# The expert gather's first chunks in PSUM banks B, and the one-hot slots ahead of three low parts

## The chip, the cores and the metric

The kernel runs on one core of a Trainium2 chip. The metric is the device time of one execution in microseconds (us); lower is better. A core has five engines that run side by side, each through its own list of instructions in order: TensorE (PE in the profile; its weight loads are listed apart as PEld), VectorE (DVE), ScalarE (ACT), GpSimd (POOL) and SyncE (SP), which here issues the DMAs that bring the weights. They wait for one another through semaphores. Products of PE land in PSUM, which has eight banks of 128 partitions x 512 fp32 numbers.

## What is computed

Two layers over 256 tokens of width 1024: gated linear attention in the first, differential attention in the second, and after either a mixture of 16 experts with a two-level router:

```python
g_idx = argmax(t @ w_group + b_group)               # one of 4 groups for each token
top_w, top_i = top_k(softmax(e_logits[g_idx]), 2)   # 2 of its 4 experts
for e in range(16):
    hdn = silu(t @ w_gate[e]) * (t @ w_up[e])       # 1024 -> 512
    y = y + combine[:, e:e + 1] * (hdn @ w_down[e]) # 512 -> 1024
h = layer_norm(ALPHA * h + y)
```

## The kernel before, in words

The change lies in the mixture of experts, `moe(layer, ...)`, which runs once for each layer. The 256 tokens lie in two blocks of 128 partitions. The router's comparisons give each token its place in each expert's list (`posm`). An expert gets 64 slots; a later, short block takes what doesn't fit (in layer 1 one such block runs as a seventeenth expert, with its slots beside those of group 3).

**One-hot slots.** For each group of four experts, `one_hot(g)` (L515) compares `posm` with a row of numbers and makes `OH`, a 0/1 matrix of 128 tokens x 256 slots for each of the two token blocks: two DVE instructions.

**Split.** The tokens' activations `xa` are used as a sum of two parts of lower precision. `split_x(k)` (L529) makes them for one chunk `k` of 128 columns: ACT copies the high part into half of a tile `xs` (L534), DVE subtracts it from `xa` for the low part (L535). There are four `xs` tiles; chunk 4 takes the tile of chunk 0 when the products of chunk 0 are done.

**Gather.** `gather_group(g)` (L538) multiplies: for each of the 8 chunks four products (L553), high part with block 0's and block 1's slots, then low part with both, add up to 128 columns x 256 slots of the gathered, transposed tokens. Two chunks (k = 0 and 1, 2 and 3, ...) share one PSUM bank. Then the pair is scaled and shifted out of PSUM into `xg`: the even chunk by DVE (L562), the odd one by ACT (L560). ACT's evacuation of a pair waits for DVE's. In group 3 of layer 1 a chunk has 320 columns (the seventeenth expert's slots too) and takes a bank alone; L558 is its extra evacuation.

**Banks.** PSUM's eight banks are shared out by name: four `pA` hold the output sums `y` through the whole loop; two `pB` and two `pC` go round. Before the change the gather takes `pC` alone, so its third pair waits until the first pair is evacuated. In the loop over experts `pB` takes the gate/up products (`gu_part`, L610) and half of the down products (`down_part`, L638); `pC` takes the other half, and the small transposes of `s_prep` (L594) and `tr_part` (L626), whose results DVE copies out (L597, and `ht` at L629) and ACT reads once more (L600). A bank is given again to whoever asks next, when the reader of its last content is done.

**Order.** The first group is gathered at the start of `moe`, right behind the router; groups 1 to 3 at experts 4, 8 and 12, behind the transposes of the expert before. Their `OH` and the split of their first four chunks are made ahead; chunks 4 to 7 are split inside the gather. The framework's scheduler orders each engine's list; `after(x)` holds an instruction behind another. At the start the code says four `split_x`, then `one_hot(0)`, `gather_group(0)`, then `combine()` (the experts' weights, a chain of small DVE instructions and one exponential on ACT). The weights come through a ring of 16 tiles `W`; a tile's next load is issued by SP when PE has used it. L181 are products with zeros that keep PE busy, and L670 adds an expert's result to `y`.

Of the kernel before, what the change touches and what calls it, by code (L numbers as in the profile page):

```python
# [43 lines left out]
def body(ctx, tc, x, w_in, wa_out, kv_w, wq, wb_out, wg, wu, wd, gate2, rows, rtab, lng, lnb, cblob, pblob, onehot, out):  # L44
    nc = tc.nc
    pe, act, dve, pool, sp = nc.tensor, nc.scalar, nc.vector, nc.gpsimd, nc.sync
# [10 lines left out]
    def nm(s):  # L57
        uid[0] += 1
        return f"{s}{uid[0]}"
# [4 lines left out]
    def pB():  # L64
        return psum.tile([128, 512], F32, tag="B", bufs=2, name=nm("pB"))

    def pC():
        return psum.tile([128, 512], F32, tag="C", bufs=2, name=nm("pC"))

    def sm(shape, tag, dt=F32, bufs=2):  # L70
        return small.tile(shape, dt, tag=tag, bufs=bufs, name=nm(tag))
# [218 lines left out]
    def spare_tile(i, shape, dt, name):  # L290
        return spare.tile(shape, dt, tag=f"x{i}", bufs=1, name=name)
# [177 lines left out]
    def moe(layer, M, lg, rstd, nr, fold, side=None):  # L469
        with tc.tile_pool(name=f"moe{layer}", bufs=1) as mp:  # L470
# [42 lines left out]
            after = lambda i: tc.issue_after(getattr(i, "ins", i)) if i is not None else contextlib.nullcontext()  # L513

            def one_hot(g):  # L515
                n = 5 if layer and g == 3 else 4
                OH[g] = mp.tile([128, 2, n, 64], F32R, tag="OH", bufs=2, name=nm("OH"))
                for b in range(2):
                    mm = dve.tensor_tensor(OH[g][:, b, 0:4],
                                      posm[:, b, 4 * g:4 * g + 4].unsqueeze(2).broadcast_to([128, 4, 64]),  # L520
                                      iota.unsqueeze(1).broadcast_to([128, 4, 64]), op=ALU.is_equal)
                    if n == 5:
                        dve.tensor_scalar(OH[g][:, b, 4], iota, extra[1][:, b:b + 1], None, op0=ALU.is_equal)
                return mm
            gcol, bcol = P_G + 16 * layer, P_B + 16 * layer

            lows = []

            def split_x(k, eng, hold=None):  # L529

                t = mp.tile([128, 2, 2, 128], F32R, tag="xs", bufs=4, name=nm("xs"))
                x_ = xa[:, :, k * 128:k * 128 + 128]
                with after(hold):
                    act.activation(t[:, 0], x_, AF.Copy)  # L534
                lows.append(eng.tensor_sub(t[:, 1], x_, t[:, 0]))  # L535
                return t

            def gather_group(g, hold=None, xs=()):  # L538

                n = 5 if layer and g == 3 else 4  # L540
                t = mp.tile([128, KC, 256], F32, tag="xg", bufs=1, name=nm("xg"))
                if n == 5:
                    tx = spare_tile(1, [128, KC, 64], F32, "xg4")
                    xg_tiles[4] = tx
                xs = list(xs)
                for k in range(KC):
                    if n == 5 or k % 2 == 0:
                        p = pC()
                    if k >= len(xs):
                        xs.append(split_x(k, dve, hold))  # L550
                    o = p[:, 0:320] if n == 5 else p[:, k % 2 * 256:k % 2 * 256 + 256]
                    for q in range(4):
                        pe.matmul(o, xs[k][:, q // 2, q % 2], OH[g][:, q % 2].rearrange("p e s -> p (e s)"), start=q == 0, stop=q == 3)  # L553
                    for i in range(k, k + 1) if n == 5 else (k - 1, k) if k % 2 else ():
                        src = p[:, 0:256] if n == 5 else p[:, i % 2 * 256:i % 2 * 256 + 256]
                        gc, bc = (pb[:, c + i:c + i + 1] for c in (gcol, bcol))
                        if n == 5:
                            dve.tensor_scalar(tx[:, i], p[:, 256:320], gc, bc, op0=ALU.mult, op1=ALU.add)  # L558
                        if n == 5 or i % 2:
                            act.activation(t[:, i], src, AF.Identity, scale=gc, bias=bc)  # L560
                        else:
                            dve.tensor_scalar(t[:, i], src, gc, bc, op0=ALU.mult, op1=ALU.add)  # L562
                xg_tiles[g] = t
# [173 lines left out]
            def overflow(left, base, rev):  # L737
# [18 lines left out]
                ht, _ = tr_part(act_part(p, 2), 2)  # L756
                scatter(st, down_part(wdn, ht, wsx, 2)[0], True)

            xs0 = [split_x(k, dve) for k in range(4)]
            act.activation(sm([128, 2], "warm"), xs0[3][:, 0, 0, 0:2], AF.Exp, scale=0.0)  # L760
            one_hot(0)
            gather_group(0, None, xs0)
            with after(lows[3]):
                cw = combine()
            prev = None
            for e in range(E + layer):
                g = min(e // 4, 3)
                if e in (4, 8, 12):
                    with after(held[e][1]):
                        one_hot(g)  # L770
                    gather_group(g, held[e][0])
# [3 lines left out]
                p = pB()  # L775
# [50 lines left out]
            if layer == 0:  # L826
                p = pB()
# [187 lines left out]
    for j in range(2):  # L1015
# [9 lines left out]
        else:  # L1025
            t = mp.tile([128, 2, 4, S], F32R, tag="xhi", name="ogT1")
# [8 lines left out]
    def mask():  # L1035
        pool.memset(late["T"][0:64, :, 192:256], 1e30)

    moe(0, M0, *rt_, mask)


    with tc.tile_pool(name="mix1", bufs=1) as mp:
# [111 lines left out]
        xt1 = lambda h, b: xtq[:, b] if h else mp.tile([128, 4, 128], F32, tag="sc", bufs=2, name=nm("xts"))  # L1153
        rt_ = out_norm(mp, 1, late["o"], lambda k: (ohi[:, k], olo[:, k]), lambda k: gsub[:, 0:1], xt1)
    moe(1, M1, *rt_)


# [60 lines left out]
```

## Time and profile before

| | us |
|---|---|
| median of 3 runs (769.76 to 772.49) | 770.43 |
| the profiled execution | 771.24 |
| its span, first to last instruction | 769.3 |
| PE busy / DVE busy / ACT busy | 727.1 / 357.4 / 296.8 |

A row of a timeline gives start, duration, engine, line, what is written and read, how many instructions are merged, and in brackets the idle time before and who ended it. A row `x14` of products is 14 issued back to back; its duration runs from the first start to the last end. A 64-column product of an expert appears twice in the trace (`x2` for one row of the program). "PEclk" is the granted share of TensorE's full clock.

### The profile page before, as it was taken

How to read it: one execution, taken by the hardware profiler on the slowest of the kernel's cores; microseconds unless marked ns; L12 is line 12 of the kernel's file. 1: busy time of each engine (PE TensorE's matmuls, PEld its weight loads, DVE VectorE, ACT ScalarE, POOL GpSimd, SP SyncE). 2: the span in 40 equal slices, each digit the busy share in tenths (PEclk: the TensorE clock that was granted, in tenths of full speed). 3: DMA queues.
4: the chain of work that ended last, by engine and by line, in shares of the span. 5: the costliest groups of instructions: out<-in, count | busy, mean ns of one | idle time of the engine just before them, and what ended most of it. 6: DMA issues, size and time to landing. Idle time of an engine off the chain costs nothing. (4 is left out here: it accounts for less than half of the span.)

```text
span 769.3 us, 10560 instructions
## 1 busy us (share of the span) xinstructions
PE 727.1 (95%) x3743; PEld 407.8 (53%) x3743; DVE 357.4 (46%) x959; ACT 296.8 (39%) x651; POOL 8.9 (1%) x21
## 2 busy tenths in 40 slices
PE   7999998999999999999999999999999999999993
PEld 5898776434333434434798877753343343343331
DVE  3655766333263332322758877654235332332225
ACT  4554766323212322222666656552232232232123
POOL 2200000000000000000000000000000000000000
PEclk9999999999999999999999999999999999999997
DMA  7999957599999999999999355619999999999951
GB/s 226 312 384 388 337 191 262 181 397 394 367 387 392 393 396 395 393 393 367 290 364 359 111 174 209 220 62 389 394 381 395 393 363 384 395 395 393 392 200 55
DMA packets 131934, 247.57 MB, mean 322 GB/s; under 512 B 7932, under 2 KB 38117, under 8 KB 131750
## 3 DMA queue, kind: packets, MB, share of 16 engines
q1 hardware_dynamic: 131270, 244.68, 87.6%
q0 software_dynamic: 176, 1.59, 0.5%
q8 instruction: 31, 0.51, 0.3%
q10 hardware_dynamic: 432, 0.59, 0.2%
q14 instruction: 25, 0.20, 0.1%
HBM read 245.77 MB, written 2.63 MB: 323 GB/s over the span
## 5 line engine op out<-in xcount | busy, mean ns | idle before, releaser
L610 PE MATMUL pB<-W,xg 128*64 128x512 f32 x1056 | 263.6, 600 | 0.0
L610 PEld LDWEIGHTS pB<-W,xg 128*64 128x64 f32 x1056 | 77.3, 138 | 137.9 <-issue 132.3
L638 PE MATMUL pB<-W,ht 128*64 128x512 f32 x248 | 112.6, 594 | 0.0
L638 PE MATMUL pC<-W,ht 128*64 128x512 f32 x248 | 111.5, 592 | 0.0
L647 DVE SCALAR_TENSOR_TENSOR o<-pB,wst,o 64x512 fp32r<-64x512 f32 x31 | 23.1, 744 | 145.3 <-ACT o L646 145.3
L119 DVE TENSOR_TENSOR lo<-W,hi 128x512 fp32r<-128x512 f32 x96 | 66.4, 696 | 37.0 <-PE pA L128 23.9
L118 ACT ACTIVATE hi<-W 128x512 fp32r<-128x512 f32 x96 | 59.3, 629 | 48.3 <-PE pA L129 27.8
L646 ACT ACTIVATE o<-pB,wst 64x512 fp32r<-64x512 f32 x31 | 21.2, 682 | 129.6 <-PE pC L638 101.8
L619 DVE TENSOR_TENSOR hd<-sl,pB 128x256 f32<-128x256 f32 x33 | 13.9, 421 | 102.5 <-ACT sl L617 102.5
L617 ACT ACTIVATE sl<-pB 128x256 f32<-128x256 f32 x33 | 12.7, 385 | 126.0 <-PE pB L610 126.0
L638 PEld LDWEIGHTS pB<-W,ht 128*64 128x64 f32 x248 | 33.3, 137 | 52.4 <-issue 49.3
L553 PE MATMUL pC<-OH,xs 128*128 128x256 f32 (+1 forms) x256 | 39.7, 308 | 7.4 <-DVE ht L629 3.8
L670 PE MATMUL pA<-o,st 128*128 128x512 f32 x132 | 40.9, 431 | 4.3 <-DVE o L664 2.1
L553 PEld LDWEIGHTS pC<-OH,xs 128*128 128x128 f32 x256 | 34.8, 203 | 17.8 <-DVE ht L629 5.2
L638 PEld LDWEIGHTS pC<-W,ht 128*64 128x64 f32 x248 | 33.9, 137 | 19.4 <-issue 18.2
L670 PEld LDWEIGHTS pA<-o,st 128*128 128x128 f32 x132 | 22.4, 191 | 33.3 <-issue 23.5
L129 PE MATMUL pA<-x1Thi,lo 128*128 128x256 f32 x128 | 36.1, 288 | 1.4 <-DVE lo L119 1.2
L127 PE MATMUL pA<-x1Thi,hi 128*128 128x256 f32 x128 | 36.7, 288 | 0.0
L128 PE MATMUL pA<-x1Tlo,hi 128*128 128x256 f32 x128 | 36.2, 284 | 0.0
L128 PE MATMUL pA<-lo,xThi 128*128 128x384 f32 (+1 forms) x96 | 34.3, 357 | 0.0
L129 PE MATMUL pA<-hi,xTlo 128*128 128x384 f32 (+1 forms) x96 | 34.3, 357 | 0.0
L127 PE MATMUL pA<-hi,xThi 128*128 128x384 f32 (+1 forms) x96 | 34.2, 362 | 0.0
(338 smaller groups left out, 1086.2 us busy)
## 6 DMA issues: line engine op xcount, KB each, us to landing
W<-in_moe_w_gate_dram SPq DMA_DIRECT2D x132, 512.0 KB, 11.2
W<-in_moe_w_up_dram SPq DMA_DIRECT2D x132, 512.0 KB, 11.0
W<-in_moe_w_down_dram SPq DMA_DIRECT2D x66, 1024.0 KB, 12.0
W<-in_a_w_in_dram SPq DMA_DIRECT2D x16, 256.0 KB, 5.6
W<-in_a_w_in_dram SPq DMA_DIRECT2D x4, 1024.0 KB, 17.8
W<-in_a_w_out_dram SPq DMA_DIRECT2D x4, 1024.0 KB, 14.4
W<-in_kv_w_dram SPq DMA_DIRECT2D x4, 1024.0 KB, 8.8
W<-in_b_w_q_dram SPq DMA_DIRECT2D x16, 256.0 KB, 5.4
```

Source lines behind the costliest of these rows:

```text
L118: act.activation(hi, src, AF.Copy)
L119: dve.tensor_sub(lo, src, hi)
L127: pe.matmul(o, l[0], r[0], start=first, stop=False, skip_group_check=skip)
L128: pe.matmul(o, l[0], r[1], start=False, stop=False, skip_group_check=skip)
L129: pe.matmul(o, l[1], r[0], start=False, stop=last, skip_group_check=skip)
L553: pe.matmul(o, xs[k][:, q // 2, q % 2], OH[g][:, q % 2].rearrange("p e s -> p (e s)"), start=q == 0, stop=q == 3)
L610: mm = pe.matmul(p[c * m:c * m + m, 0:2 * fw].rearrange("p (g f) -> p g f", g=2), xg(k), w[:, :, kk, c * fw:c * fw + fw], start=k == 0, st ...
L619: anchor[1] = dve.tensor_mul(h, sl, p[:, fw:2 * fw])
L638: mm = pe.matmul(p[2 * c // nt][c * m:c * m + m, 0:w], ht[:, q % n, (q // n) * m:(q // n) * m + m], wd_[q // 2][:, q % 2, c * w:c * w + w] ...
L646: act.activation(hi, src, AF.Copy, scale=ws[a:a + m, 0:1])
L647: dve.scalar_tensor_tensor(lo, src, ws[a:a + m, 0:1], hi, op0=ALU.mult, op1=ALU.subtract)
L670: mm = pe.matmul(y[b][c], st[:, b * 128:b * 128 + 128], o[c], start=False, stop=last, skip_group_check=True)
```

## The change

Two edits. The gather takes its banks in turn: pairs 0 and 1 in `pB`, pairs 2 and 3 in `pC` (in the wide group chunks 0, 1 in `pB`, 2, 3 in `pC`, 4, 5 in `pB`, 6, 7 in `pC`). And at the start of `moe` only chunk 0 gets its low part ahead; the low parts of chunks 1 to 3 are made after both halves of `OH`.

```diff
-            def split_x(k, eng, hold=None):
+            def split_x(k, eng, hold=None, later=False):
...
-                lows.append(eng.tensor_sub(t[:, 1], x_, t[:, 0]))
+                low = lambda: lows.append(eng.tensor_sub(t[:, 1], x_, t[:, 0]))
+                if later:
+                    return t, low
+                low()
                 return t
...
                 for k in range(KC):
                     if n == 5 or k % 2 == 0:
-                        p = pC()
+                        i = k if n == 5 else k // 2
+                        p = pC() if i // 2 % 2 else pB()
...
-            xs0 = [split_x(k, dve) for k in range(4)]
+            xs0, rest = [split_x(0, dve)], []
+            for k in range(1, 4):
+                t, low = split_x(k, dve, later=True)
+                xs0.append(t)
+                rest.append(low)
             act.activation(sm([128, 2], "warm"), xs0[3][:, 0, 0, 0:2], AF.Exp, scale=0.0)
-            one_hot(0)
+
+            with after(one_hot(0)):
+                for low in rest:
+                    low()
             gather_group(0, None, xs0)
```

The lists of PE, DVE and ACT change in the eight gathers and nowhere else; those of SP and POOL stay as they were. Line numbers move: L553 becomes L558, L560 L565, L562 L567, L610 L615.

DVE at the start of layer 0's experts, behind `posm` (`xs` rows are low parts, `mx`, `ex`, `comb` belong to `combine`). Before:

```order
L519 TENSOR_TENSOR OH_1710<-posm_1694,cb 128x256
L535 TENSOR_TENSOR xs_1696<-xa,xs_1696 128x256
L535 TENSOR_TENSOR xs_1699<-xa,xs_1699 128x256
L535 TENSOR_TENSOR xs_1702<-xa,xs_1702 128x256
L535 TENSOR_TENSOR xs_1705<-xa,xs_1705 128x256
L519 TENSOR_TENSOR OH_1710<-posm_1694,cb 128x256
L568 TENSOR_REDUCE mx_1770<-lg_1645 128x10
L570 TENSOR_TENSOR ex_1772<-lg_1645,mx_1770 128x40
L574 SCALAR_TENSOR_TENSOR comb_1775<-rank_1681,ex_1772 128x32
L578 TENSOR_REDUCE s_1779<-ex_1772 128x2
L576 TENSOR_REDUCE sg_1777<-comb_1775 128x8
L535 TENSOR_TENSOR xs_1737<-xa,xs_1737 128x256
```

And now:

```order
L519 TENSOR_TENSOR OH_1707<-posm_1694,cb 128x256
L535 TENSOR_TENSOR xs_1696<-xa,xs_1696 128x256
L519 TENSOR_TENSOR OH_1707<-posm_1694,cb 128x256
L535 TENSOR_TENSOR xs_1699<-xa,xs_1699 128x256
L535 TENSOR_TENSOR xs_1701<-xa,xs_1701 128x256
L535 TENSOR_TENSOR xs_1703<-xa,xs_1703 128x256
L573 TENSOR_REDUCE mx_1770<-lg_1645 128x10
L567 TENSOR_SCALAR xg_1713<-pB_1714,pb 128x256
L575 TENSOR_TENSOR ex_1772<-lg_1645,mx_1770 128x40
L567 TENSOR_SCALAR xg_1713<-pB_1725,pb 128x256
L535 TENSOR_TENSOR xs_1737<-xa,xs_1737 128x256
```

The second half of `OH` stands three low parts earlier, and chunk 4's low part (`xs_1737`) now stands behind the evacuations of both first pairs instead of ahead of them; most of `combine` moves behind all low parts.

PE at expert 4 of layer 0, from the transposes of expert 3 on (L553 is the gather, L610 the gate/up product of expert 4). Before:

```order
L594 MATMUL pC_1999<-ident_r,ohw_1996 128x128 x2
L626 MATMUL pC_2006<-ident_r,hd_1990 128x128 x2
L553 MATMUL pC_2015<-OH_2011,xs_2016 128x256 x4
L553 MATMUL pC_2015<-OH_2011,xs_2023 128x256 x4
L553 MATMUL pC_2032<-OH_2011,xs_2033 128x256 x4
L553 MATMUL pC_2032<-OH_2011,xs_2040 128x256 x4
L610 MATMUL pB_2083<-W_992,xg_2014 64x512
L553 MATMUL pC_2049<-OH_2011,xs_2050 128x256 x4
L553 MATMUL pC_2049<-OH_2011,xs_2057 128x256 x4
```

And now:

```order
L599 MATMUL pC_1999<-ident_r,ohw_1996 128x128 x2
L631 MATMUL pC_2006<-ident_r,hd_1990 128x128 x2
L558 MATMUL pB_2015<-OH_2011,xs_2016 128x256 x4
L558 MATMUL pB_2015<-OH_2011,xs_2023 128x256 x4
L558 MATMUL pB_2032<-OH_2011,xs_2033 128x256 x4
L558 MATMUL pB_2032<-OH_2011,xs_2040 128x256 x4
L558 MATMUL pC_2049<-OH_2011,xs_2050 128x256 x4
L558 MATMUL pC_2049<-OH_2011,xs_2057 128x256 x4
L558 MATMUL pC_2066<-OH_2011,xs_2067 128x256 x2
L615 MATMUL pB_2083<-W_992,xg_2014 64x512
L558 MATMUL pC_2066<-OH_2011,xs_2067 128x256 x2
```

The first four chunks write `pB`, and the expert's first product, which stood behind chunk 3, now stands in the middle of chunk 6 and takes the `pB` bank in which chunks 0 and 1 were added up.

## Rows read from the trace of the kernel before

**Rows 1.** The page, busy time of the engines over the span.
```profile
PE 727.1 (95%) x3743; PEld 407.8 (53%) x3743; DVE 357.4 (46%) x959; ACT 296.8 (39%) x651; POOL 8.9 (1%) x21
```

**Rows 2.** PE's waits over the whole span: us in total, times, longest.
```profile
PE pC L553 <- DVE ht L629: 3.8, 6, 0.6
PE pC L553 <- DVE OH L519: 2.2, 2, 1.1
...
PE pC L553 <- ACT xg L560: 1.3, 3, 0.6
```

**Rows 3.** Timeline of PE at the start of layer 0's experts.
```profile
134.27 3.36 PE L553 MATMUL pC<-OH,xs 128*128 128x256 f32 x14 [1.12 <-DVE OH L519]
...
138.65 2.18 PE L553 MATMUL pC<-OH,xs 128*128 128x256 f32 x16
140.75 7.08 PE L610 MATMUL pB<-W,xg 128*64 128x512 f32 x30
```

**Rows 4.** Timeline of DVE at the same place.
```profile
132.46 1.42 DVE L535 TENSOR_TENSOR xs<-xa,xs 128x256 fp32r<-128x256 f32 x4
133.80 0.41 DVE L519 TENSOR_TENSOR OH<-posm,cb 128x256 fp32r<-128x256 f32 x1
...
136.17 0.54 DVE L562 TENSOR_SCALAR xg<-pC,pb 128x256 f32<-128x256 f32 x1
...
140.59 0.48 DVE L591 TENSOR_SCALAR ohw<-OH,comb 128x128 f32<-128x128 f32 x2
```

**Rows 5.** Stretches: length, PE, PEld, DVE, ACT, POOL busy, PEclk, DMA share, GB/s.
```profile
134.00:138.00 4.00, 3.73 (x15) 3.25 (x16) 2.21 (x9) 1.76 (x5) 0.00 (x0) 0.57 0.00 0
232.00:239.00 7.00, 5.09 (x17) 1.99 (x14) 3.30 (x5) 2.43 (x5) 0.00 (x0) 1.00 1.05 393
506.00:510.00 4.00, 4.00 (x16) 2.70 (x15) 2.62 (x9) 2.68 (x7) 0.00 (x0) 0.57 0.00 0
608.00:612.00 4.00, 3.09 (x10) 2.17 (x12) 2.05 (x4) 0.85 (x3) 0.00 (x0) 0.57 1.03 400
656.00:660.00 4.00, 4.00 (x12) 1.50 (x13) 0.70 (x3) 1.40 (x3) 0.00 (x0) 0.57 1.02 408
```

**Rows 6.** Timeline of PE at the start of layer 1's experts.
```profile
505.71 3.00 PE L553 MATMUL pC<-OH,xs 128*128 128x256 f32 x14 [1.10 <-DVE OH L519]
...
512.19 1.08 PE L610 MATMUL pB<-W,xg 128*64 128x512 f32 x4
```

**Rows 7.** Timeline of PE at expert 4 of layer 0.
```profile
187.55 2.18 PE L553 MATMUL pC<-OH,xs 128*128 128x256 f32 x16 [0.63 <-DVE ht L629]
189.71 1.07 PE L610 MATMUL pB<-W,xg 128*64 128x512 f32 x2
190.72 2.17 PE L553 MATMUL pC<-OH,xs 128*128 128x256 f32 x16
192.82 0.65 PE L610 MATMUL pB<-W,xg 128*64 128x512 f32 x2
```

**Rows 8.** Timeline of ACT at expert 4 of layer 0.
```profile
188.33 1.38 ACT L534 ACTIVATE xs<-xa 128x256 fp32r<-128x256 f32 x3 [0.55 <-PE pC L553]
189.69 0.57 ACT L560 ACTIVATE xg<-pC,pb 128x256 f32<-128x256 f32 x1
```

**Rows 9.** Timeline of PE at expert 12 of layer 0.
```profile
308.88 2.18 PE L553 MATMUL pC<-OH,xs 128*128 128x256 f32 x16 [0.58 <-ACT xg L560]
```

**Rows 10.** Timeline of PE at expert 12 of layer 1 (320 columns).
```profile
683.02 1.44 PE L553 MATMUL pC<-OH,xs 128*128 128x320 f32 x8 [0.63 <-DVE ht L629]
...
691.73 0.64 PE L610 MATMUL pB<-W,xg 128*64 128x512 f32 x1
```

**Rows 11.** Layer 0's last expert weights: issue on SP, its landing (us last), use on PE.
```profile
340.42 0.60 SPq L282 DMA_DIRECT2D W<-in_moe_w_up_dram  x1
...
W<-in_moe_w_up_dram SPq DMA_DIRECT2D x1, 512.0 KB, 10.8
...
354.41 3.17 PE L610 MATMUL pB<-W,xg 128*64 128x512 f32 x14
```

## The prediction

> **What bounds the kernel now.** I read the page first: PE is busy for 727.1 us, 95% of the span, VectorE for 46% and ScalarE for 39% [rows 1]. So a change pays only where PE stands or runs slowly. The list of PE's waits comes next. The gather (L553) stands in it three times: six waits of up to 0.63 us for `ht`, two of 1.1 us for the second half of the one-hot slots, three for ScalarE's evacuation, 7.3 us together [rows 2]. The timelines of the eight gathers then show how the time passes around these waits, and the granted clock of short stretches whether PE ran at full rate.
>
> At the start of layer 0's experts PE issues two products, stands for 1.12 us until the second half of `OH` is there, does 14 products in 3.36 us, 0.24 us each, and later 16 in 2.18 us, 0.136 each [rows 3]. The difference is the clock: from 134 to 138 us the mean granted share is 0.57, a stretch at 1.2 instead of 2.4 GHz. Layer 1 shows the same share at the same place [rows 5], and a pause of 1.10 us [rows 6]. What keeps PE waiting stands in VectorE's list: between the two halves of `OH` it makes four low parts, 132.46 to 133.80 us, 0.335 us each [rows 4].
>
> At expert 4 the gather takes a C bank, and both hold the small transposes until VectorE has copied `ht`: PE stands for 0.63 us. Its chunks 4 to 7 then need the C banks of chunks 0 to 3 back. In between lies the expert's first product (two rows of the trace) [rows 7].
>
> **The change part by part.** Nothing is added or removed: the same products, subtractions and evacuations run; eight gathers are reordered. SP's and POOL's lists are the same, no DMA is moved. Durations are those of the profiled execution, 771.24 us with 1.94 us around its span of 769.3; the median of the runs is 0.81 us lower.
>
> *The starts of the two expert stages.* Three of four low parts go behind the second half of `OH`: it is there 3 x 0.335 = 1.0 us earlier, and PE's pause shrinks to about 0.1 us. The low parts of chunks 1 to 3 then come every 0.335 us, while PE needs four products of 0.136, or 0.54 us, for a chunk: PE doesn't wait for them. If the clock stays at full rate, the 14 products take 14 x 0.136 = 1.9 us. Then a new wait arises. Chunk 4's low part now stands behind the evacuation of pair 1 on VectorE, which can begin only when chunk 3 is done: 0.54 us for the evacuation, 0.335 for the low part and some 0.25 for the two hand-overs, 1.1 us in all. PE has two high-part products (0.27) and the expert's first product (30 rows in 7.08 us, so 0.47 for its two) [rows 3] to do in it, and stands for about 0.4; I take 0.5. The remainder is then 1.9 + 16 x 0.136 + 0.47 + 0.5 = 5.05 us. Before, it took from 134.27 to 140.75, 6.48 us [rows 3], and from 505.71 to 512.19, also 6.48 [rows 6]. So 1.0 + 1.43 = 2.4 us per layer, 4.9 for both. Bounds: 1.0 each if only the earlier slots count, 2.9 if the new wait is nothing.
>
> *Experts 4 and 8 of both layers.* The first pair takes the B bank that the gate/up products left; VectorE read it for `hd`, which the transposes ahead had to wait for anyway. So the 0.63 us go, and nothing is late in their place. Inside, from 187.55 to 192.82, 5.27 us pass [rows 7] with 32 x 0.136 + 0.47 = 4.82 of work: 0.45 us of waits for the first pairs' evacuations. Those go too, because chunks 4 and 5 take a C bank free since `ht`. The expert's first product now needs chunk 0's and 1's bank back: ScalarE begins that evacuation 2.14 us after the gather's first product, behind three high-part copies (188.33 to 189.69), and ends it by 2.71 [rows 8]; the product comes after 26 others, at 3.5 us. Its cover is 0.8 us. I take 1.05 of the 1.08, four times: 4.2. Bounds 0.63 and 1.08 each.
>
> *Expert 12, layer 0.* The 0.63 us and 0.58 us for ScalarE's evacuation [rows 9] go. No expert product stands between here, so chunk 7's low part, behind the evacuation of chunks 4 and 5 on VectorE, comes some 0.35 late: 0.86. Bounds 0.6 and 1.2.
>
> *Expert 12, layer 1.* Here each chunk fills a bank, and chunk 2 had to wait for chunk 0's. From the start of the first wait, 683.02 - 0.63 = 682.39, to 691.73 pass 9.34 us; 32 products of 0.18 (1.44 / 8) and three expert products of 0.47 are 7.17 [rows 10]. Of 2.17 idle, about 0.4 stay, since ScalarE copies chunk 7's high part behind the evacuation of chunk 5: 1.8. Bounds 0.63 and 2.17.
>
> *What costs nothing.* The chain of `combine` moves behind the low parts. Its first user, the scaling at 140.59 us [rows 4], is needed when the 30 expert products end, 140.75 + 7.08 [rows 3]: 7 us of cover, 4.8 if these end 2.4 earlier. Without it PE would wait for it as long as it is late.
>
> *Weights.* The stream of loads runs at 393 to 408 GB/s in the experts' stretches of [rows 5] and could be what is late next. Layer 0's last gate/up tile is issued at 340.42 and lands 10.8 later, at 351.2; its first product is the seventh of the 14 rows from 354.41 in 3.17 us, at 355.8 [rows 11]. That leaves 4.5 us. The start's 2.4 us shift the loads too, since the ring was full and waited for PE; only 1.05 + 1.05 + 0.86 = 3.0 come later and eat into the 4.5. So the gain passes on.
>
> **The sum.** 4.9 + 4.2 + 0.86 + 1.8 = 11.8 us: 759.5 against the profiled execution, 758.7 against the median. I take 759.0.
>
> **The rivals.**
> 1. *The clock falls at the starts all the same.* For: PE still pauses ahead of the gather, for the router's chain. Against: in layer 0 nearly all of the idle time just before the fall is the 1.12 us that go. Then the 14 products keep some 0.24 us each, 1.4 us more per layer: 759.0 + 2.9 = 762. The Trainium skill (TensorE: Matmul & The Clock Gate, "A second HAM failure mode: psum-queue depth-cycling") says that short idles between groups of products, as these cycle through PSUM banks, are enough to make the clock fall again and again; that is this rival. The trace agrees that pauses near 1 us can do it [rows 3, 5], and shows layer 0 at expert 5 keep the full clock with 1.9 of 7 us idle, where layer 1 lost it at its like place, 608 us [rows 5]; so a pause alone doesn't decide.
> 2. *The waits change their name.* The inner waits come back as waits for low parts, since VectorE works strictly in its list's order and evacuations now stand ahead; only the named first waits go: 2 x 1.0 + 6 x 0.63 = 5.8, so 765. For: chunk 4's low part moved back at the starts. Against: at experts 4 to 12 the low parts of chunks 4 and 5 stay ahead of the second evacuation.
> 3. *Slower: the expert's first product waits for its bank.* In seven gathers it now takes chunk 0's and 1's bank and holds all later products behind it. If ScalarE empties it as late as all its copies and other pairs, PE stands. It decides from 3.5 us after the gather's start; over 3.5 + 11.8 / 7 = 5.2 us the kernel is slower than before. At 6 us the price is 7 x 2.5 = 17.5, so 776. Against: 2.71 us by [rows 8].
> 4. *The weights bind.* If the loads don't shift with the start, layer 0 keeps 4.5 us of its 5.4: about 760, inside the forecast.
> 5. *Nothing happens*, 770.4, because what ends the waits is something else. Against: both lists of [rows 2 to 4] name the very instructions that are moved.
>
> **How the numbers follow.** The forecast, 756 to 761.5, has 0.68. Rival 1 has 0.13, rival 2 0.12, rival 3 0.04, rival 5 0.03. Two more stretches at half rate stand at 608 and 656 us [rows 5]; either is worth up to (1 - 0.57) x 4 = 1.7 us if it is gone by chance, or as much if another comes. So the range begins at 755.5 and reaches over rival 1 to rival 2 at 765. About 0.5%, 3.9 us, is what a measurement of this kernel can tell from no change: faster means below 766.6. That holds for the forecast and rivals 1 and 2: 0.92 (a little taken off for mixtures); same 0.04; slower 0.04.
>
> **What would show it.** Right: no row of L558 waiting for `ht`; the wait for `OH` at 0.2 us or less; the clock at 1.00 in the 4 us after either start; 14 products in 1.9 us; expert 4's gather within 5 us from first to last product. Wrong: a wait of L615 on `xg` L565 over 0.3 us in several gathers (rival 3), L558 on `xs` L535 over 0.4 us (rival 2), a share of 0.57 behind either start (rival 1), PE waiting for `W`. A time above 766.6 would mean that the gathers' idle time wasn't what bound the start of the experts.

## The result and the profile after

| | before | after |
|---|---|---|
| median, us | 770.46 (4 runs, 769.76 to 772.49) | 759.80 (4 runs, 758.06 to 760.02) |
| profiled execution / its span, us | 771.24 / 769.3 | 759.6 / 757.9 |

The ratio is 0.9854, with a 95% interval of 0.9842 to 0.9866: faster by 11.2 us by the ratio and by 10.7 between the medians, where 11.4 were forecast from the median. A later comparison, on another occasion (five runs of the changed kernel), gave 0.9853 (0.9835 to 0.9871).

The page after, busy time of the engines; it answers to [rows 1]:

```profile
PE 722.3 (95%) x3743; PEld 406.3 (54%) x3743; DVE 356.5 (47%) x959; ACT 294.4 (39%) x651; POOL 8.9 (1%) x21
```

PE is busy for 4.8 us less with the same number of instructions, and the span is 11.4 us shorter: the rest, 6.6 us, is time in which PE stood. Of PE's and its loader's waits, after, these have to do with the gather; they answer to [rows 2]:

```profile
PE pB L615 <- ACT xg L565: 0.3, 2, 0.2
...
PE pB L558 <- DVE OH L519: 0.2, 1, 0.2
...
PEld pC L558 <- DVE xs L535: 5.3, 8, 0.8
```

No row has the gather waiting for `ht` or for ScalarE's evacuation any more, and the 2.2 us for `OH` are 0.2. The loader waits for low parts, 5.3 us in eight times; six of them, 0.81 us each, lie in the time in which PE does the expert's lone product, and PE's own list has no such row. Nor has it one for `W`, so the weights don't bind. PE at the start of layer 0's experts, after, which answers to [rows 3]:

```profile
134.25 0.47 PE L558 MATMUL pB<-OH,xs 128*128 128x256 f32 x2
134.87 1.93 PE L558 MATMUL pB<-OH,xs 128*128 128x256 f32 x14 [0.15 <-DVE OH L519]
136.64 0.40 PE L558 MATMUL pC<-OH,xs 128*128 128x256 f32 x2
137.20 1.07 PE L615 MATMUL pB<-W,xg 128*64 128x512 f32 x2 [0.16 <-ACT xg L565]
138.20 1.94 PE L558 MATMUL pC<-OH,xs 128*128 128x256 f32 x14
140.07 7.08 PE L615 MATMUL pB<-W,xg 128*64 128x512 f32 x30
```

Three things are to be read off. The pause is 0.15 us instead of 1.12; the 14 products take 1.93 us instead of 3.36; and the single product of the expert (`x2`, two rows of the trace) takes 1.07 us, not the 0.47 that the prediction gave it. PE at expert 4 of layer 0, after, which answers to [rows 7]:

```profile
185.83 0.38 PE L631 MATMUL pC<-ident_r,hd 128*128 128x128 f32 x2
185.97 2.16 PE L558 MATMUL pB<-OH,xs 128*128 128x256 f32 x16
187.97 1.39 PE L558 MATMUL pC<-OH,xs 128*128 128x256 f32 x10
189.28 1.07 PE L615 MATMUL pB<-W,xg 128*64 128x512 f32 x2
190.28 0.98 PE L558 MATMUL pC<-OH,xs 128*128 128x256 f32 x6
191.19 1.50 PE L615 MATMUL pB<-W,xg 128*64 128x512 f32 x5
```

The transposes ahead of it, before:

```profile
186.54 0.38 PE L626 MATMUL pC<-ident_r,hd 128*128 128x128 f32 x2
```

The gather's first product starts 0.14 us behind the transposes' start. In the trace of before that distance is 1.01 us (186.54 to 187.55), so the first wait was worth 0.87 us, more than the 0.63 that its row names. The row counts idle time from the modelled end of the last product; when nothing waits, the next product starts before that end. From the gather's first product to the row behind the gather it is 5.22 us (185.97 to 191.19) against 5.27 before: inside, almost nothing came of it.

The wide gather of layer 1, after, which answers to [rows 10]:

```profile
673.16 1.42 PE L558 MATMUL pB<-OH,xs 128*128 128x320 f32 x8
674.42 1.34 PE L558 MATMUL pC<-OH,xs 128*128 128x320 f32 x8
675.59 1.34 PE L558 MATMUL pB<-OH,xs 128*128 128x320 f32 x8
676.76 0.95 PE L558 MATMUL pC<-OH,xs 128*128 128x320 f32 x4
677.65 1.07 PE L615 MATMUL pB<-W,xg 128*64 128x512 f32 x2
678.65 0.86 PE L558 MATMUL pC<-OH,xs 128*128 128x320 f32 x4
```

And three rows of before, behind the first row of [rows 10]:

```profile
684.91 1.64 PE L553 MATMUL pC<-OH,xs 128*128 128x320 f32 x8 [0.45 <-ACT xg L560]
686.79 0.85 PE L553 MATMUL pC<-OH,xs 128*128 128x320 f32 x4 [0.25 <-ACT xg L560]
...
689.95 1.08 PE L610 MATMUL pB<-W,xg 128*64 128x512 f32 x4
```

PE does the gather without a wait between chunks: the first two groups of eight products take 1.26 and 1.17 us from start to start, where they took 1.89 and 1.88 (683.02 to 684.91 to 686.79). One product of the expert stands among them where three stood before, a lone one and two issued together (`x4`).

### The profile page after: what moved, and what is told of

Same layout as the page of the kernel before. It is cut to its first block, busy times and chain, and to the rows that moved or that the text cites. A ratio compares the mean times of both kernels' runs of the same rounds, so it can differ in the third digit from the quotient of the medians.

```text
span 757.9 us, 10570 instructions
## 1 busy us (share of the span) xinstructions
PE 722.3 (95%) x3743; PEld 406.3 (54%) x3743; DVE 356.5 (47%) x959; ACT 294.4 (39%) x651; POOL 8.9 (1%) x21
## 5 line engine op out<-in xcount | busy, mean ns | idle before, releaser
L615 PE MATMUL pB<-W,xg 128*64 128x512 f32 x1056 | 262.8, 599 | 0.3 <-ACT xg L565 0.3
L615 PEld LDWEIGHTS pB<-W,xg 128*64 128x64 f32 x1056 | 77.2, 137 | 138.3 <-issue 131.3
L605 ACT ACTIVATE pC<-pC 128x256 f32<-128x256 f32 x33 | 12.1, 368 | 41.0 <-DVE st L602 40.3
L129 PEld LDWEIGHTS pA<-x1Thi,lo 128*128 128x128 f32 x128 | 24.1, 191 | 3.2 <-DVE lo L119 2.6
## 6 DMA issues: line engine op xcount, KB each, us to landing
W<-in_moe_w_gate_dram SPq DMA_DIRECT2D x132, 512.0 KB, 11.2
W<-in_moe_w_up_dram SPq DMA_DIRECT2D x132, 512.0 KB, 11.2
```

Of the source, the lines that this page charges most:

```text
L129: pe.matmul(o, l[1], r[0], start=False, stop=last, skip_group_check=skip)
L615: mm = pe.matmul(p[c * m:c * m + m, 0:2 * fw].rearrange("p (g f) -> p g f", g=2), xg(k), w[:, :, kk, c * fw:c * fw + fw], start=k == 0, st ...
```

## The experiments

Theory A is the prediction's: the banks pay at experts 4, 8 and 12, the order of slots pays at the two starts, and there the pause is what brings the clock down. The others (B to G) are stated with the kernels that test them. "The start" below is the time from the gather's first product of layer 0 to the end of the first expert's run of gate/up products; the traces of layer 1 give the same within 0.05 us unless the clock differs. Before it is 15.19 us (132.64 to 147.83), after 12.90 (134.25 to 147.15).

| kernel | median, us | ratio to before, 95% | mean granted clock | the start, us |
|---|---|---|---|---|
| banks alone | 762.35 | 0.9892 (0.9876 to 0.9908) | 0.987 | 13.81 |
| slots alone | 769.96 | 0.9991 (0.9982 to 1.0) | 0.988 | 14.20 |
| pause filled | 770.53 | 0.9993 (0.9984 to 1.0003) | 0.987 | |
| wide gather in C | 761.91 | 0.9879 (0.9864 to 0.9894) | 0.989 | 12.90 |
| before, second profile | 771.24 (one run) | | 0.985 | 13.87 |
| expert held | 755.25 | 0.9795 (0.9774 to 0.9816) | 0.992 | 13.00 |
| pair together | 752.38 | 0.977 (0.9748 to 0.9792) | 0.989 | 12.07 |
| slots alone, held | 765.83 | 0.9942 (0.9917 to 0.9967) | 0.988 | 13.00 |
| pair, and the pause | 756.86 | 0.9821 (0.9799 to 0.9843) | 0.989 | 13.70 |
| pair and blocks | 752.23 | 0.9762 (0.9743 to 0.9781) | 0.988 | 12.06 |
| after, again | 759.50 | 0.9853 (0.9835 to 0.9871) | 0.989 | 12.90 |

The mean granted clock is that of all executions of a kernel; 21 executions of before have 0.985. It is a mean over the span, in which each stretch at half rate shows.

**Banks alone.** The kernel before, with

```diff
-                        p = pC()
+                        i = k if n == 5 else k // 2
+                        p = pC() if i // 2 % 2 else pB()
```

> The kernel before with the change of banks alone; the one-hot slots and low parts at the starts stand as before. Theory A (the banks pay at experts 4, 8 and 12, the slots at the two starts): experts 4 and 8 give 0.95 us each in both layers, expert 12 1.2 and 2.4, together 7.4; at the starts PE still waits 1.1 us for the second half of the slots and the clock is still at 0.57 behind it: 763.0 (762 to 764.6). Rival B (the starts also gain by the banks, since the waits inside the gather were what kept the clock down): 14 products at the starts in 1.9 us and 760 to 761. In both no wait of the gather for ht is left.

Measured: 762.35, inside A's range, but not by A's account of the starts. Experts 4, 8 and 12 gained as forecast from the changed kernel's trace. At the start neither theory held. PE, with the banks alone:

```profile
132.56 0.47 PE L555 MATMUL pB<-OH,xs 128*128 128x256 f32 x2
134.20 1.93 PE L555 MATMUL pB<-OH,xs 128*128 128x256 f32 x14 [1.16 <-DVE OH L519]
...
139.29 7.08 PE L612 MATMUL pB<-W,xg 128*64 128x512 f32 x30
```

The pause is as long as before, and yet the 14 products run at full rate, in both layers. PE had done the same as in [rows 3] until then. So the pause does not by itself bring the clock down, and B's reason falls too: the fall of [rows 3] comes before the gather's inner waits.

**Slots alone.** The changed kernel with `p = pC()` in the gather again.

> The changed kernel with the gather back in the C banks alone: only the order of slots and low parts at the two starts is new. Theory A: the pause goes (1.0 us) and with it the fall of the clock (14 products in 1.9 instead of 3.4 us), 2.3 us per layer, nothing at experts 4 to 12: 765.9 (765 to 767.5). Rival C (the clock falls at the starts whatever the pause): 1.0 per layer, 768.5. Rival B: under 1 us per layer, since without the free banks the gather stands inside: 769 or more.

Measured: 769.96, a gain of 0.2% at most. The clock stayed up and the pause went, but the start is 14.20 us. PE:

```profile
132.73 2.55 PE L556 MATMUL pC<-OH,xs 128*128 128x256 f32 x16
135.21 1.07 PE L613 MATMUL pB<-W,xg 128*64 128x512 f32 x2
136.22 1.45 PE L556 MATMUL pC<-OH,xs 128*128 128x256 f32 x10
137.60 1.07 PE L613 MATMUL pB<-W,xg 128*64 128x512 f32 x2
138.60 0.74 PE L556 MATMUL pC<-OH,xs 128*128 128x256 f32 x4
139.27 1.07 PE L613 MATMUL pB<-W,xg 128*64 128x512 f32 x2
...
140.71 6.22 PE L613 MATMUL pB<-W,xg 128*64 128x512 f32 x26
```

The order now puts three single products of the expert between the gather's, where one stood, and each takes 1.07 us: more than the pause gave back. The two edits need one another. Against the start of the kernel before at full clock (13.87, below) the banks alone give 0.06 us, the slots alone lose 0.33, both together give 0.97.

**Pause filled.** The kernel before with four more products of zeros:

```diff
-            warm(3, mm)
+            warm(7, mm)
```

> The kernel before with 7 instead of 3 products of zeros behind the router's last product, which fill some 1.0 us of the pause; slots, low parts and banks as before. It tells the price of the clock from that of the pause. Theory A: the gather goes on at the same time as before (the wait for the second half of the slots decides), but the clock stays at 1.00 and the 14 products take 1.9 instead of 3.4 us: 1.4 us per layer, 767.6 (767 to 768.5). Rival C: share 0.57 all the same, 770.5 or a little slower.

Measured: 770.53, unclear against before. The clock was at 1.00 at both starts and the 14 products took 1.94 us, as A says, but a fall at 32 us, before the experts, and others at 237, 609 and 657 us stood against it. The four products filled only half of the pause (0.55 us are left, not 0.1), and the gather begins 0.7 us later by them, so its start isn't in the table. One profile of each can't tell what a kernel does to the clock; the next run shows why.

**Before, a second profile.** No edit.

> The kernel before, unchanged, for a second profiled execution. Theory A (the 1.1 us pause at the starts brings the clock down each time): share 0.57 behind both starts again. Theory G (the clock falls in a few of the many places where PE is not dense, and which ones is chance; the pause is one such place): full clock behind at least one start, where the 14 products take 1.9 us, and stretches at half rate at other places instead, such as 33 or 235 us.

PE at both starts, in this second execution of the kernel before (layer 0, then layer 1), and the granted clock of stretches, its columns as in [rows 5]:

```profile
134.14 0.48 PE L553 MATMUL pC<-OH,xs 128*128 128x256 f32 x2
135.77 1.94 PE L553 MATMUL pC<-OH,xs 128*128 128x256 f32 x14 [1.15 <-DVE OH L519]
...
140.93 7.08 PE L610 MATMUL pB<-W,xg 128*64 128x512 f32 x30
```

```profile
506.87 3.33 PE L553 MATMUL pC<-OH,xs 128*128 128x256 f32 x14 [1.10 <-DVE OH L519]
```

```profile
32.00:36.00 4.00, 4.00 (x14) 3.22 (x15) 2.17 (x5) 0.63 (x1) 0.13 (x1) 0.57 1.14 321
134.00:138.00 4.00, 2.71 (x18) 2.23 (x18) 3.55 (x14) 2.91 (x7) 0.00 (x0) 1.00 0.02 4
...
506.00:510.00 4.00, 3.13 (x14) 3.03 (x14) 2.49 (x10) 1.87 (x6) 0.00 (x0) 0.62 0.02 4
```

The same kernel, with the same pause, keeps the full clock at layer 0's start this time, and loses it at layer 1's and at 32 us. That is as G says: over the thirteen profiles taken, the clock falls at one to four of six places (near 33, 134, 236, 506, 605 and 653 us, beside the kernel's end), and at which ones changes from execution to execution. The price of a fall at a start can be read off: 15.19 - 13.87 = 1.32 us.

**Wide gather in C.** The changed kernel with `p = pC() if n == 5 or i // 2 % 2 else pB()`.

> The changed kernel, with the wide gather of layer 1's expert 12 back in the C banks. Theory A: the 0.63 us for ht and the waits of each second chunk for its bank come back, 2.4 us: 762.2 (761.5 to 763). Rival D (of the 2.4 us only the first wait is the bank's, the rest is chance of the clock near 656 us): 0.6 to 0.9 us, 760.6.

Measured: 761.91, 2.1 to 2.4 us more than the changed kernel's two medians; in the traces 2.44, all of it at this gather. Rival D falls; A's term stands.

**Expert held.** The changed kernel, in which `gather_group` returns its last product, and

```diff
-                with after(prev and prev[4]):
+                with after(gm if e % 4 == 0 and e < E else prev and prev[4]):
                     mm = gu_part(M[e][0], (0,), xg, p, 2)
```

> The changed kernel with the expert's first products held until the gather's last product. In the changed kernel the expert's first product stands alone among the gather's products and takes 1.0 us, where the run of 30 takes 0.47 each. Theory E (alone it cannot overlap with its partner of the other 64 columns, so it costs 0.5 too much): 0.4 us less at each of experts 4 and 8 and at the wide expert 12, about nothing at the starts, where PE would wait for chunk 4's low part instead: 757.9. Rival F (it fills a wait for low parts that PE would have anyway): 0 to 0.4 us more in each gather, 760 to 762.

Measured: 755.25, more than E asked. The traces lose 0.1 us at each start (13.00 against 12.90), give 0.66 us at each of experts 4 and 8, and 0.1 at the wide one, 2.5 in all; the remaining 1.7 to 2.0 goes with the mean clock, 0.992 against 0.989 (a fall at 603 us in the changed kernel's profile, which this one doesn't have, is worth 1.6 alone). The end of the first gather and the first expert's run, with the expert held (in the changed kernel 30 rows took 7.08 us, above):

```profile
136.34 0.40 PE L558 MATMUL pC<-OH,xs 128*128 128x256 f32 x2
137.48 1.76 PE L558 MATMUL pC<-OH,xs 128*128 128x256 f32 x12 [0.73 <-DVE xs L535]
...
139.86 7.09 PE L616 MATMUL pB<-W,xg 128*64 128x512 f32 x32
```

At the start PE now stands 0.73 us for chunk 4's low part, in the place of the lone product. 32 rows take as long as 30. Products of 64 columns run two and two, and an odd one costs what two cost.

**Pair together.** The expert's first two products (both halves of the columns, first chunk) are issued inside the gather at the place of the one, in seven gathers:

```diff
                     for q in range(4):
-                        pe.matmul(o, xs[k][:, q // 2, q % 2], ...)
+                        if pair and pair[0:2] == (k, q):
+                            first = pair[2](t)
+                        with after(first):
+                            pe.matmul(o, xs[k][:, q // 2, q % 2], ...)
...
+            gather_group(0, None, xs0, (4, 2, pair_of(0)))
```

> The changed kernel with the expert's first two products (both halves of the columns of chunk 0) side by side at the place where the first stands now, and the gather's later products behind both; in seven gathers. Theory E: the pair takes hardly longer than the one product (1.0 us), and one of 0.47 us is saved behind the gather: 7 x 0.45 = 3.1 us, 756.7. Rival F (two products there take twice 1.0 us): 7 x 0.5 slower, 763.

Measured: 752.38, beyond E, and rival F is out. PE at the start of layer 0, and at expert 4:

```profile
135.60 1.08 PE L618 MATMUL pB<-W,xg 128*64 128x512 f32 x4 [0.16 <-ACT xg L568]
136.61 1.94 PE L561 MATMUL pC<-OH,xs 128*128 128x256 f32 x14
138.48 6.23 PE L618 MATMUL pB<-W,xg 128*64 128x512 f32 x28
```

```profile
186.83 1.08 PE L618 MATMUL pB<-W,xg 128*64 128x512 f32 x4
```

The pair takes 1.08 us where the single product took 1.07, and the run behind it is 0.85 us shorter (6.23 against 7.08). By the start times in the trace it is 0.80 to 0.87 us at each of the seven gathers, 5.9 in all, of the 6.4 between the two ratios (0.9853 and 0.977 of 771). The price in the expectation, 0.45, was too low, because an odd product is lost twice: 15 of them need eight turns, 14 need seven. The Trainium skill (TensorEngine Tiling (Array Packing), "Key Properties") says that tiles of the array operate independently and can work in parallel; by that a lone tile leaves the other half of the array unused, and these rows agree (1.07 and 1.08 us).

**Slots alone, held.** The kernel with slots alone and the expert held as above.

> The kernel with the new order of slots alone (gather in the C banks), and the expert's first products held until the gather's last. There the three products of the first expert stood alone in the gather at each start, 1.07 us each, and the pause's gain of 1.0 us did not come through. Theory E: held, they cost 0.47 each; the gather itself then waits for its low parts, of which some 0.5 us per layer stay: 0.5 to 1.2 us less than with the slots alone per layer, 768 to 769; at experts 4 and 8 another 0.3 less each, 767. Rival F: the waits for low parts and banks come in their place, 770.

Measured: 765.83, 4.1 us less than the slots alone and below E's 767. In the traces experts 4 and 8 give 1.6, the wide gather 0.6, and the start falls from 14.20 to 13.00, 1.2 us per layer, the upper end of E. So it is the three lone products that ate the gain of the slots.

**Pair, and the pause.** The pair together, with `xs0` and `one_hot(0)` in the old order.

> The kernel with the pair of expert products together, and the old order of slots and low parts at the starts (the 1.1 us pause) back; banks as changed. It tells what the pause costs, with its clock. By the traces so far the pause itself is 0.9 us per layer, 1.8 for both. Theory A (each pause brings the clock down, 1.33 us): 4.5 us more than with the pair alone, 757. Theory G (the pause is only one of many places at which the clock may fall; by the mean granted clock over the executions of the kernels with and without it, 0.987 against 0.989, it costs 0.4 us a start on average): 1.8 + 0.8 = 2.6 us more, 755.2, and a mean clock of 0.988 or above, not 0.984.

Measured: 756.86, just what A says, and yet A is wrong here: a pause need not bring the clock down. PE and the granted clock at the start of layer 0, and the clock at that of layer 1:

```profile
135.66 1.94 PE L561 MATMUL pB<-OH,xs 128*128 128x256 f32 x14 [1.16 <-DVE OH L519]
...
138.61 1.08 PE L618 MATMUL pB<-W,xg 128*64 128x512 f32 x4 [0.78 <-ACT xg L568]
```

```profile
134.00:138.00 4.00, 2.65 (x18) 2.26 (x18) 3.56 (x13) 2.90 (x7) 0.00 (x0) 1.00 0.02 4
...
500.00:504.00 4.00, 2.39 (x18) 2.17 (x20) 3.55 (x14) 2.90 (x9) 0.00 (x0) 1.00 0.02 4
```

The clock stays up at both starts, and its mean is that of the pair alone. The time went elsewhere: in this order the pair, fixed in its place, waits 0.78 us for its bank, so the pause costs 1.63 us per layer (13.70 - 12.07), 3.3 for both. The spans of the two profiles differ by 3.1 us and the medians by 4.5; what is over of these is found in no trace. G's size of the pause (0.9) missed; its statement on the clock held.

**Pair and blocks.** The two small products of `blocks()` moved from between the third and fourth product of expert 2 to behind the fourth (the call stands at `e == 2`, behind the first `gu_part`).

> The kernel with the pair together, and also the two products of blocks() (L685 there, one call per layer), which stand between the third and the fourth product of expert 2, moved behind the fourth. Theory E (expert products run two and two, and an odd number before a break costs as much as the next even one): 0.86 us per layer, 1.7 us, 751. Rival F (the odd product is not lost, since it pairs with the first down product): 0.

PE at expert 2 of layer 0, with the pair alone, and then with the blocks moved:

```profile
158.36 1.93 PE L618 MATMUL pB<-W,xg 128*64 128x512 f32 x6
160.22 0.39 PE L685 MATMUL pC<-sel,ones 128*128 128x16 f32 x2
160.54 0.64 PE L618 MATMUL pB<-W,xg 128*64 128x512 f32 x1
160.54 0.64 PE L646 MATMUL pB<-W,ht 128*64 128x512 f32 x1
```

```profile
158.89 1.94 PE L618 MATMUL pB<-W,xg 128*64 128x512 f32 x8
160.76 0.39 PE L685 MATMUL pC<-sel,ones 128*128 128x16 f32 x2
```

Eight rows take what six took, and by the end of expert 2 the trace is 0.84 us ahead, in both layers: E. The median, 752.23, doesn't show the 1.7 us; the intervals overlap, and the mean clock is 0.988 against 0.989. In the trace a fall at 232 us takes 1.3 us of it back, and the experts start 0.5 us later. So the place is shown, the total isn't.

**After, again.** No edit.

> The changed kernel, unchanged, beside the same runs of the kernel before. Ratio 0.985 again; full clock behind both starts in the second profiled execution (no pause, so neither theory A nor G expects a fall there often), mean granted clock 0.989 against 0.985.

Measured: 0.9853; full clock at both starts; the stretches at half rate stood at 235 and 648 us, where the first profile had 33 and 603.

## Why the prediction was right, and where its reasons were not

| term | forecast, us | in the traces, us |
|---|---|---|
| the two starts | 2 x 2.4 | 2 x 0.97, and 2 x 1.32 where the clock had fallen |
| experts 4 and 8 | 4 x 1.05 | 4 x 0.92 (0.87 first wait, 0.05 inside) |
| expert 12, layer 0 | 0.86 | 1.18 (0.87 and 0.31) |
| expert 12, layer 1 | 1.8 | 2.44 (0.87, 1.34 by the chunks' waits, 0.23 around the expert's products) |
| sum | 11.8 | 9.24 without the clock, 11.88 with the falls at the starts |

*The starts.* The step that failed is that the pause brings the clock down ("nearly all of the idle time just before the fall is the 1.12 us that go"), by which a further 1.43 us per layer was counted as sure. The same pause stood ahead of a full clock at both starts with the banks alone, at both with the pair and the pause, and at one of the four starts of the two profiles of before; ahead of a fall at the other three. In the eight profiles without the pause none of the sixteen starts has a fall: the pause may be needed for one there, but it isn't enough. The size of a fall was right (1.32 against 3.36 - 1.9), its certainty wasn't. What the two edits give there without the clock is 0.97 us, and it takes both: the 1.0 us of earlier slots alone is eaten by odd products of the expert. The new wait, taken at 0.5 us, shows only with the expert held, 0.73 us: its path, put at 1.1 us with 0.25 for hand-overs that no row of before shows, takes 1.14 there (136.34 to 137.48). In the changed kernel PE does the lone product in that time, which takes 1.0 instead of 0.47.

*The clock.* Its mean rose from 0.985 to 0.989. Of the 11.2 us measured, 9.2 are found in the gathers; the other 2 are what the clock can account for (of the 21 executions of before those at 0.982 stand near 772.3 us, those at 0.986 near 770.0). In the two profiles the falls at the starts are worth 2.64 us, and before has one more at 656 us, 1.6; the changed kernel has one at 33 us, 1.6, and loses 0.6 more by that at 603 than before by that at 608. That leaves 2.0, which with the 9.24 makes 11.3 of the 11.4 between the spans. So it is in part luck that 759.8 came so near to 759.0. Why before is at 0.985 and every other kernel higher, also those with the pause, is not settled.

*Rival 1* (the clock falls all the same) didn't come in either profile of the changed kernel. The rule of the Trainium skill on short idles that was weighed with it (TensorE: Matmul & The Clock Gate, "A second HAM failure mode: psum-queue depth-cycling") is borne out in part: falls do come at such pauses, but they came and went there with the idles unchanged.

*Experts 4 and 8.* Total nearly right (0.92 against 1.05) from two errors that cancel: the first wait is 0.87, not 0.63, and the 0.45 of "waits inside" wasn't a wait. It was the expert's lone product, priced at 0.47 from a run of 30, which takes 1.0 before and after the change alike. For the same reason one sign of being right was missed: expert 4's gather takes 5.2 us, not 5 at most. *Expert 12:* both undersized, by the same 0.24 us of the first wait. In layer 1 the 2.44 is above even the bound of 2.17: products of 320 columns, priced at 0.18 us from a row of eight, take 0.146 from start to start (674.42 to 675.59), so that more of the 9.34 us was waiting than the 2.17 that it found, though the three expert products took 0.6 more than their price.

*What was to cost nothing* cost nothing: PE doesn't wait for `combine`'s scaling, and for the bank that ScalarE empties it waits 0.16 us at a start, so rival 3 stayed away. Rival 2 left its mark, the loader's 5.3 us for low parts, but PE did the expert's product meanwhile. The time lies well below 766.6, above which the gathers' idle time would not have been what bound the start of the experts.

## What to carry to other kernels

A run's mean price per product holds only inside the run: look up what a product costs where it stands alone, and keep products of half the columns in even numbers before each break. A stall that disappears with its clock fall must be measured in several executions, with the stall put back, before the clock is counted as its price; here a total agreed with the wrong reason. Two edits that each remove a wait can be worth next to nothing apart, as at the starts here, where the scheduler filled the place of one with work that costs more.

## What was not expected of the hardware

- One 64-column product of 512 by itself takes 1.07 us, two 1.08 us; 30 rows of the trace (15 products) 7.08, 32 rows 7.09.
- The granted clock falls at places that change from execution to execution of one kernel: 134, 506, 608 and 656 us in the first profile of before, 32, 237, 507 and 657 in the second; a fall at a start of the experts costs 1.32 us.
- A wait that its row puts at 0.63 us was worth 0.87: without it, the next product starts 0.14 us behind the start of the products ahead of it, while these still run.

The fastest kernels tried are the pair together (752.38 us, 0.977 of before) and the pair with the blocks moved (752.23); both are below the changed kernel's 759.5 to 759.8.
